# Moving the operands of a split fp32 product to one common place in their 512-byte blocks

## The chip, the cores and the metric

The kernel runs on one core of a Trainium2 chip. The metric is device time in microseconds (us) of one execution. A core has TensorE (PE; its weight loads are listed as PEld), VectorE (DVE), ScalarE (ACT), GpSimd (POOL), and the DMA queues, most of which SyncE (SP) issues to here. SBUF, the on-chip memory, has 128 partitions; a tile takes the same range of bytes in each of them, and "place" here means where in its partition's bytes a tile begins, counted within blocks of 512 bytes.

## The reference, cut to what matters

Two layers work on 256 latent tokens `x` and 256 context tokens `ctx`, with 1024 features. Layer 0 is retention and a dense SwiGLU on all 512 tokens; layer 1 is gated linear attention (GLA) and a mixture of experts on the latent tokens alone, two of eight experts for each token. All is fp32.

```python
h_l = rmsnorm(lat, norm_mix_g[i]) * (1.0 + sc1_l) + sh1_l
...
f = swiglu(h_all, ffn_w_gate[j], ffn_w_up[j], ffn_w_down[j])       # layer 0, width 2816
f = moe_swiglu(h_all, moe_w_router[j], moe_w_gate[j], moe_w_up[j], moe_w_down[j])   # layer 1, 8 x 3584
...
def swiglu(h, w_gate, w_up, w_down):
    return (jax.nn.silu(h @ w_gate) * (h @ w_up)) @ w_down
```

## The kernel before

**A product.** An fp32 product is made of three products of another 4-byte type (fp32r). Each operand is split into a high part and the rest: `whi` and `wlo` of a weight tile, `hh` and `hl` of the normed tokens, `ah` and `al` of the hidden layer, and so on. `mm3` (L87 to L89) issues high x high, high x low and low x high into one PSUM bank. In each, the stationary operand has 128 columns (512 bytes of a partition) and the moving one mostly 512 columns (2048 bytes), sometimes 256.

**A weight tile.** Each 1 MB tile is loaded on SP's queue into a `raw` buffer (`wraw`, L61), cast into `whi` by ScalarE (L79) and subtracted into `wlo` by VectorE (L80), both in `wsplit`. There are four `raw` buffers (in the expert stage three more, tag `more`, and some borrowed places), three `whi` and three `wlo`. The order of the engines' work is the order in which the program issues it; a few lists of pieces (`weave`, `todo`, `ada_beat`) put small work between the products.

**The stages**, by the profiled span: conditioning and retention up to about 412 us, the dense feed-forward up to about 813, GLA up to about 1010, routing, and from about 1047 us the experts (`moe`). An item of the expert loop is one expert and 512 of its 3584 hidden columns: six weight tiles, 72 products, and four transposes (L1417). In the experts' products the weights are the moving operand and the gathered tokens (`hh` or `xb`) or `ah`, `al` the stationary one; in retention and the feed-forward it is mostly the other way round. Tokens of two experts at a time are gathered by products with a one-hot matrix (L1372), and an expert's result goes back by products with `yy` and `GG` (L1460).

**Where tiles lie.** The pools take memory in the order in which their tiles are first asked for; each tile is rounded up to 32 bytes. `cp` and `wp` lie at the bottom, then come the pools of the stage (`rp` retention, `fp` feed-forward, `gp` and `gc` GLA, `mp` and `xp` experts), one after the other over the same bytes. `ap`, with `x0`, `x1`, `hh`, `hl` in that order, stands at the upper end and is pushed down by whatever is added to it. `gap` (L34) asks for a tile that nothing uses. With `reuse_waits="tile"`, the first writer of a tile waits for the last readers of just those tiles whose bytes it takes over.

The sizes of the tiles, added up in this order, give the place of each operand of a split product:

| operand | stage | byte of its block before |
|---|---|---|
| `raw`, `whi`, `wlo` | all | 96 |
| `raw` buffers of tag `more` (no product reads them) | experts | 320 |
| `hh`, `hl`, and over them `xb`, `spare`, GLA's gated outputs | all | 480 |
| `GG`, `yy` (over `x0`, `x1`) | experts | 480 |
| `vh`, `vl`, `pch`, `pcl`, `qh`, `ql`, `kh`, `kl`, `ol` | retention | 96 |
| `plh`, `pll`, `oh` | retention | 224 |
| `ah`, `al` | feed-forward | 480 |
| `ah`, `al` | experts | 480 |
| `th`, `tl` | experts | 224, 352 |
| `wa`, `wuh`, `aT` | GLA | 480 |

Of the kernel before, what the change touches and what calls it, by code (L numbers as in the profile page):

```python
# [8 lines left out]
F32 = mybir.dt.float32  # L9
F32R = mybir.dt.float32r  # L10
# [3 lines left out]
P = 128  # L14
D = 1024
KT = D // P
# [10 lines left out]
def tile_hybrid(ctx: ExitStack, tc: tile.TileContext, a, out):  # L27
# [4 lines left out]
    state = {"pieces": 2}  # L32

    def gap(pool, nbytes):  # L34

        pool.tile([P, nbytes // 4], F32, name=f"gap{state.setdefault('gaps', 0)}")
        state["gaps"] += 1


# [50 lines left out]


    gap(cp, 32)
    tp = ctx.enter_context(tc.tile_pool(name="tp", bufs=3))
    pro = ExitStack()
# [32 lines left out]
    ap = act.enter_context(tc.tile_pool(name="ap", bufs=1, side="right", reuse_waits="tile"))  # L127
    xs = [ap.tile([P, KT, 256], F32, tag=f"x{i}", name=f"x{i}") for i in range(2)]
    hh = ap.tile([P, KT, NTOK], F32R, name="hh")
    hl = ap.tile([P, KT, NTOK], F32R, tag="hl", name="hl")  # L130
    vecT = cp.tile([P, 128], F32, name="vecT")
    wrt = cp.tile([P, KT, 8], F32, name="wrt")
    adabT = cp.tile([P, 96], F32, name="adabT")
# [6 lines left out]

    def gain(layer, which, base_col, A=None, ks=slice(0, KT), streams=2):

        A = A or cp.tile([P, KT, 2], F32, name=f"A{layer}{which}")
        n = ks.stop - ks.start
        g = vecT[:, base_col + ks.start:base_col + ks.stop].unsqueeze(2).to_broadcast([P, n, streams])
        sc = mods[layer][:, which * 24 + 8 + ks.start:which * 24 + 8 + ks.stop, :streams]
        nc.vector.scalar_tensor_tensor(A[:, ks, :streams], sc, 1.0, g, OP.add, OP.mult)
        return A

# [111 lines left out]
    class Norm:  # L261


        def __init__(self, layer, which, A, stream):
            self.layer, self.which, self.A, (self.s, self.sl) = layer, which, A, stream
            self.adder = nc.gpsimd
# [110 lines left out]
    with ExitStack() as ph:  # L377
# [29 lines left out]
        A = cp.tile([P, KT, 2], F32, name="A00")  # L407
# [15 lines left out]
        pro.close()  # L423
        edge = Boundary(0, 1, 32, STREAMS[::-1])
        retention(tc, nc, a, locals(), new_ps, wsplit, wraw, rows, mm3, add_gated)
        edge2 = Boundary(1, 0, 24, STREAMS)
        ffn(tc, nc, a, locals(), new_ps, wsplit, rows, mm3, add_gated)
        tail = gla(tc, nc, a, locals(), new_ps, wsplit, rows, mm3, add_gated)
        moe(tc, nc, a, out, locals(), new_ps, wsplit, rows, mm3)
        act.close()  # L430

# [19 lines left out]
def retention(tc, nc, a, env, new_ps, wsplit, wraw, rows, mm3, add_gated):  # L451
# [3 lines left out]
    with ExitStack() as ph:  # L455
        rp = ph.enter_context(tc.tile_pool(name="rp", bufs=1, reuse_waits="tile"))
# [197 lines left out]
        state = env["state"]  # L654
# [14 lines left out]
        for _ in steps:  # L669
            pass  # L670
        nc.sync.dma_start(rope, a["k_rope"])
        env["gap"](rp, 32)
        lg = rp.tile([P, 2, 4], F32, name="lg")
        nc.scalar.activation(lg, ld, AF.Exp)
        nc.vector.tensor_scalar(lg, lg, -1.0, None, OP.mult)
# [28 lines left out]
def ffn(tc, nc, a, env, new_ps, wsplit, rows, mm3, add_gated):  # L704
    hh, hl, tp = (env[k] for k in ("hh", "hl", "tp"))
    wg, wu, wd = (a["ffn_w_" + n][0] for n in ("gate", "up", "down"))
    with ExitStack() as ph:
        fp = ph.enter_context(tc.tile_pool(name="fp", bufs=2, reuse_waits="tile"))
        nc.sync.dma_start(env["wrt"], a["moe_w_router"][0].rearrange("(k p) e -> p k e", p=P))

        def up(c):
            ws = [wsplit(rows(w, 0, D, c * 256, 256)) for w in (wg, wu)]
            ah = fp.tile([P, 2, NTOK], F32R, tag="ah", name="ah")
            al = fp.tile([P, 2, NTOK], F32R, tag="al", name="al")
            banks = [[new_ps(), new_ps()] for _ in range(2)]
            for part, cols in enumerate([slice(0, 256), slice(256, 512)] if c == 0 else [slice(0, 512)]):
                ts = [tp.tile([P, NTOK], F32, tag="sq", bufs=2, name="t")[:, cols] for _ in range(2)]
                for n, (wh, wl) in enumerate(ws):
                    for m in range(2):
                        ms = slice(m * 128, m * 128 + 128)  # L720
                        ps, t = banks[n][m][:, cols], ts[m]
                        for kt in range(KT):
                            mm3(ps, wh[:, kt, ms], wl[:, kt, ms], hh[:, kt, cols], hl[:, kt, cols],
                                kt == 0, kt == KT - 1)
                        env["ada_beat"](5.12)
                        if c == 0 and part == 0:
                            env["edge"].after(2 * n + m)
                        if n == 0:
                            i = nc.scalar.activation(t, ps, AF.Silu)
                            if c == DFF // 256 - 1 and m == 1:  # L730
                                env["root_table"](i)
                        else:
                            nc.vector.tensor_tensor(t, t, ps, OP.mult)
                            nc.scalar.copy(ah[:, m, cols], t)
                            nc.vector.tensor_sub(al[:, m, cols], t, ah[:, m, cols].bitcast(F32))
            return ah, al

        def down(cs, acts):
            ws = [wsplit(rows(wd, c * 256, 256, 0, D)) for c in cs]
            last = len(cs) > 1  # L740
            for n, part in enumerate([[st] for st in env["edge2"].order] if last else [STREAMS]):
                cols = slice(min(sl.start for _, sl in part), max(sl.stop for _, sl in part))
                for mt in range(KT):
                    ps = new_ps()
                    ms = slice(mt * 128, mt * 128 + 128)
                    k = 2 * len(cs)
                    for ft in range(k):
                        wh, wl = ws[ft // 2]
                        ah, al = acts[ft // 2]
                        mm3(ps[:, cols], wh[:, ft % 2, ms], wl[:, ft % 2, ms], ah[:, ft % 2, cols], al[:, ft % 2, cols],  # L750
                            ft == 0, ft == k - 1)
                    env["ada_beat"](1.28)
                    add_gated(mt, ps, 0, 1, part)
                    if last:
                        env["edge2"].before(n, mt)

        prev = None
        n = DFF // 256
        for c in range(n):
            cur = up(c)  # L760
            if c == 1:
                env["ada_until"](12)
            if prev is not None and c < n - 1:
                down([c - 1], [prev])
            if c == 0:
                env["ada_plan"]([(0, c) for c in range(11, 12)] + [(1, c) for c in range(12)], 3, 2, env["edge"].second.ends[1:])
            if c == n - 1:
                env["ada_until"](0)
                down([c - 1, c], [prev, cur])
            prev = cur  # L770
# [328 lines left out]
def moe(tc, nc, a, out, env, new_ps, wsplit, rows, mm3):  # L1099
    hh, ap, tp, ident, mods = (env[k] for k in ("hh", "ap", "tp", "ident", "mods"))  # L1100
    xT = env["xs"][0]
    wrt = env["wrt"]
    E, FE, FC = 8, 3584, 512
# [7 lines left out]
    with ExitStack() as ph:  # L1111
        mp = ph.enter_context(tc.tile_pool(name="mp", bufs=1, reuse_waits="tile"))
        xp = ph.enter_context(tc.tile_pool(name="xp", bufs=2))
        env["state"]["more"] = mp
        km = mp.tile([P, 320], F32, name="km")
        xl = mp.tile([P, 2, D], F32, name="xl")
        g2b = mp.tile([P, D], F32, name="g2b")
        state = env["state"]
# [5 lines left out]
        nc.gpsimd.tensor_copy(one01, one)  # L1124


        A = env["gain"](1, 1, 40, mp.tile([P, KT, 2], F32, name="A11"), streams=1)

        aw = mp.tile([P, KT * E + 24], F32, name="aw")
        nc.gpsimd.memset(aw, 0.0)  # L1130
        nc.vector.tensor_tensor(aw[:, :KT * E].rearrange("p (k e) -> p k e", e=E), wrt,
                                A[:, :, 0:1].to_broadcast([P, KT, E]), OP.mult)
        w3 = mp.tile([P, 4, 2], F32, name="w3")
        env["gap"](mp, 64)

        def rstd():

# [42 lines left out]
                return k.ins  # L1180
            return pss, add

        th = mp.tile([P, 2, D], F32R, name="th")
        turned = []
        norm = env["Norm"](1, 1, A, STREAMS[0])
        norm.adder = nc.vector
# [62 lines left out]

        state["pieces"] = 1  # L1250
        state["ready"] = ready
        lg = mp.tile([P, 2, E], F32, name="lg")
        for tt in range(2):
            nc.vector.scalar_tensor_tensor(lg[:, tt, :], ps[:, tt * E:tt * E + E], r[:, tt:tt + 1], cb, OP.mult, OP.add)

        env["gap"](mp, 32)
        tl = mp.tile([P, 2, D], F32R, name="tl")

        def normed_high(q):

# [43 lines left out]
                                                OP.mult, OP.add).ins  # L1304
        cmax = mp.tile([1, 1], F32, name="cmax")
        cint = mp.tile([1, 1], mybir.dt.int32, name="cint")
        env["gap"](mp, 32)

        def late():
            with env["held"]([state["split"].ins, state["lost"].ins]):  # L1310
# [18 lines left out]
        env["state"]["pp"] = ph.enter_context(tc.tile_pool(name="pm", bufs=8, space=bass.MemoryType.PSUM, reuse_waits="tile"))  # L1329
        env["state"]["banks"] = 6  # L1330

        env["gap"](mp, 96)
        xs = [hh]
        GG = ap.tile([P, KT, 256], F32R, tag="x0", name="GG")

# [337 lines left out]
```

## Time and profile before

| | |
|---|---|
| median of three runs | 2074.34 us (2073.31 to 2074.95) |
| the profiled execution | 2069.22 us |
| its span, first to last instruction | 2067.5 us |
| instructions in the span | 25718 |
| PE, DVE, ACT busy | 98%, 83%, 56% of the span |
| DMA | 498.22 MB, mean 241 GB/s |

The profiled execution is one more run with the hardware profiler on. "Busy" of PE counts a product from its start to an end that is modelled: products overlap, so that 98% is not a rate. The DMA rate is about 60 to 300 GB/s in the first half of the span and about 350 GB/s in the experts' half.

### The profile page before, as it was taken

Reading aid. Unit: us, or ns where it says so; the run is one execution under the profiler, and the core shown is the slowest. Engines: PE = TensorE matmul, PEld = TensorE weight load, DVE = VectorE, ACT = ScalarE, POOL = GpSimd, SP = SyncE. Lnnn points to the kernel's source line nnn. Section 1 sums busy time; section 2 is a strip of 40 time slices with the busy share of each in tenths; the row PEclk is TensorE's granted clock in tenths of the full one; section 3 lists DMA queues with packets and bytes.
Section 4 is the critical chain, followed back from the end, with each engine's and each line's share of the span. In section 5 each row is a group of like instructions: output and inputs, shape, how many; then the busy total and the mean of one; then the engine's idle time right before and its main releaser. Section 6 shows DMA issues by size and latency. Waiting matters only on the chain.

```text
span 2067.5 us, 25718 instructions
## 1 busy us (share of the span) xinstructions
PE 2018.7 (98%) x9810; PEld 1664.8 (81%) x9810; DVE 1714.8 (83%) x2484; ACT 1162.5 (56%) x1242; POOL 113.8 (6%) x118
## 2 busy tenths in 40 slices
PE   7999999999999999999999999999999999999997
PEld 5788888888888888888878888777887778878775
DVE  5999977659999974687688888888888898888887
ACT  4643434243222223665477777767777677776765
POOL 0201010020000001100110101000000001000000
PEclk9999999999999999999999999999999999999999
DMA  9645343213546662223669899999999999999993
GB/s 286 194 152 186 125 160 102 82 62 123 169 159 222 208 208 68 87 82 104 251 231 358 292 342 356 338 345 360 352 342 345 352 354 351 347 343 358 354 351 139
DMA packets 272498, 498.22 MB, mean 241 GB/s; under 512 B 10357, under 2 KB 112173, under 8 KB 272369
## 3 DMA queue, kind: packets, MB, share of 16 engines
q1 hardware_dynamic: 270976, 495.07, 68.8%
q8 instruction: 79, 1.29, 0.3%
q0 software_dynamic: 512, 0.86, 0.1%
q10 hardware_dynamic: 880, 0.59, 0.1%
q14 instruction: 51, 0.41, 0.1%
HBM read 495.43 MB, written 1.05 MB: 240 GB/s over the span
## 4 chain that ended last, share of the span: by engine, by line
PE 89%; DVE 6%; ACT 2%; issue 1%; DMA 1%; SPq 1%; POOL 0%; ACTq 0%; DVEq 0%; POOLq 0%
PE ps L88 23%; PE ps L87 23%; PE ps L89 23%; PE y L88 5%; PE y L87 5%; PE y L89 5%; DVE wlo L80 3%; PE ps L1417 1%; PE ps L1372 1%; PE ps L975 1%; PE ps L1460 1%; SPq L155 1%; ACT whi L79 0%; PE ps L911 0%; DMA early<-in_ada_w_dram 0%
## 5 line engine op out<-in xcount | busy, mean ns | idle before, releaser
L80 DVE TENSOR_TENSOR wlo<-raw,whi 128x2048 fp32r<-128x2048 f32 (+3 forms) x515 | 933.1, 1832 | 149.1 <-ACT whi L79 145.3
L79 ACT CAST whi<-raw 128x2048 fp32r<-128x2048 f32 (+3 forms) x515 | 784.6, 1541 | 411.4 <-PE ps L88 188.0
L87 PE MATMUL ps<-hh,whi 128*128 128x512 f32 (+1 forms) x864 | 312.0, 363 | 2.1 <-ACT hh L1016 1.0
L89 PE MATMUL ps<-hh,wlo 128*128 128x512 f32 (+1 forms) x864 | 311.0, 361 | 1.7 <-DVE wlo L80 1.7
L88 PE MATMUL ps<-hl,whi 128*128 128x512 f32 (+1 forms) x800 | 292.9, 367 | 2.5 <-DVE hl L322 2.5
L87 PE MATMUL ps<-whi,hh 128*128 128x512 f32 x640 | 256.2, 400 | 1.1 <-ACT hh L321 0.9
L88 PE MATMUL ps<-wlo,hh 128*128 128x512 f32 x640 | 255.1, 399 | 1.6 <-DVE wlo L80 1.6
L214 DVE SCALAR_TENSOR_TENSOR sum<-raw,cT,sum 128x256 f32<-128x256 f32 x448 | 194.2, 484 | 0.4
L89 PEld LDWEIGHTS ps<-hh,wlo 128*128 128x128 f32 x864 | 165.6, 192 | 28.1 <-DVE wlo L80 2.9
L87 PEld LDWEIGHTS ps<-hh,whi 128*128 128x128 f32 x864 | 165.0, 192 | 28.2 <-ACT hh L321 1.5
L88 PE MATMUL ps<-wlo,xb 128*128 128x512 f32 x448 | 180.5, 403 | 3.8 <-DVE wlo L80 3.5
L88 PE MATMUL y<-wlo,ah 128*128 128x512 f32 (+1 forms) x450 | 177.4, 394 | 0.0
L89 PE MATMUL y<-whi,al 128*128 128x512 f32 (+1 forms) x450 | 177.1, 394 | 0.0
L87 PE MATMUL ps<-whi,xb 128*128 128x512 f32 x448 | 177.1, 395 | 0.0
L89 PE MATMUL ps<-whi,hh 128*128 128x512 f32 x448 | 176.7, 394 | 0.0
L89 PE MATMUL ps<-whi,xb 128*128 128x512 f32 x448 | 176.6, 394 | 0.0
L88 PEld LDWEIGHTS ps<-hl,whi 128*128 128x128 f32 x800 | 152.9, 191 | 28.5 <-DVE hl L322 3.4
L87 PE MATMUL y<-whi,ah 128*128 128x512 f32 (+1 forms) x450 | 164.4, 394 | 0.0
L88 PEld LDWEIGHTS ps<-wlo,hh 128*128 128x128 f32 x640 | 121.0, 189 | 30.1 <-DVE wlo L80 4.4
L87 PEld LDWEIGHTS ps<-whi,hh 128*128 128x128 f32 x640 | 120.8, 189 | 29.9 <-ACT hh L321 1.3
L372 DVE SCALAR_TENSOR_TENSOR x<-ps,mod,x 128x256 f32<-128x256 f32 x240 | 105.2, 477 | 37.8 <-PE ps L89 35.8
L88 PEld LDWEIGHTS ps<-wlo,xb 128*128 128x128 f32 x448 | 84.3, 188 | 28.1 <-DVE wlo L80 10.7
(373 smaller groups left out, 2860.0 us busy)
## 6 DMA issues: line engine op xcount, KB each, us to landing
raw<-in_moe_w_gate_dram SPq DMA_DIRECT2D x108, 1024.0 KB, 7.3
raw<-in_moe_w_up_dram SPq DMA_DIRECT2D x108, 1024.0 KB, 7.0
raw<-in_moe_w_down_dram SPq DMA_DIRECT2D x107, 1024.0 KB, 6.9
raw<-in_ada_w_dram SPq DMA_DIRECT2D x44, 1024.0 KB, 5.3
raw<-in_ret_w_in_dram SPq DMA_DIRECT2D x22, 1024.0 KB, 5.3
raw<-in_gla_w_in_dram SPq DMA_DIRECT2D x12, 1024.0 KB, 5.3
raw<-in_ffn_w_gate_dram SPq DMA_DIRECT2D x11, 1024.0 KB, 5.3
raw<-in_ffn_w_up_dram SPq DMA_DIRECT2D x11, 1024.0 KB, 5.4
```

What stands on the lines that cost most here:

```text
L79: state["split"] = nc.scalar.copy(hi[:, ks, ns], raw[:, ks, ns])
L80: state["lost"] = lo_engine.tensor_tensor(lo[:, ks, ns], raw[:, ks, ns], hi[:, ks, ns].bitcast(F32), OP.subtract)
L87: nc.tensor.matmul(ps, lh, rh, start=first, stop=False)
L88: nc.tensor.matmul(ps, lh, rl, start=False, stop=False)
L89: state["mm"] = nc.tensor.matmul(ps, ll, rh, start=False, stop=last).ins
L155: nc.sync.dma_start(t, rows(a["ada_w"][layer], 0, D, c0 + i * n // 2, n // 2))
L214: nc.vector.scalar_tensor_tensor(t, raw[:, k, :], w, t, OP.mult, OP.add)
L372: i = nc.vector.scalar_tensor_tensor(xs[s][:, mt, :], ps[:, sl.start - off:sl.stop - off], g, xs[s][:, mt, :], OP.mult, OP.add)
L975: nc.tensor.matmul(ps[:, h * 256:h * 256 + 256], l, v[:, j, h * 256:h * 256 + 256], start=n == 0, stop=n == 3)
L1372: nc.tensor.matmul(ps, src[:, tt, ks], G[:, tt].rearrange("p e s -> p (e s)"), start=n == 0, stop=n == 3)
L1417: nc.tensor.transpose(ps[:, k * 128:k * 128 + 128], t[:, k * 128:k * 128 + 128], ident)
L1460: nc.tensor.matmul(ps, GT[:, tt, :], ys[i][:, rs, :], start=i == 0, stop=i == 1)
```

## The change

No instruction of the kernel is taken out, added or put elsewhere. The change sets the sizes of the unused `gap` tiles and the order in which `mp`'s tiles are asked for, so that the operands of the split products begin at byte 96 of a block: `hh`, `hl`, `xb`, `GG`, `yy` by the gap behind `hl`; `plh`, `pll`, `oh` by the larger gap in `rp`; the feed-forward's `ah`, `al` by a gap ahead of them; the experts' `th`, `tl` by asking for them right behind two tables of 64 bytes; the experts' `ah`, `al` by the last gap in `mp`. The `raw` buffers of tag `more` come to byte 448; `wa`, `wuh`, `aT` stay at 480. Behind the change the last tile of `xp` ends where `ap` begins.

```diff
     def gap(pool, nbytes):
 
-        pool.tile([P, nbytes // 4], F32, name=f"gap{state.setdefault('gaps', 0)}")
+        pool.tile([P, nbytes // 4], F32, name=f"gap{state.setdefault('gaps', 0)}", bufs=1)
         state["gaps"] += 1
...
     hl = ap.tile([P, KT, NTOK], F32R, tag="hl", name="hl")
+    gap(ap, 384)
...
         nc.sync.dma_start(rope, a["k_rope"])
-        env["gap"](rp, 32)
+        env["gap"](rp, 416)
...
         fp = ph.enter_context(tc.tile_pool(name="fp", bufs=2, reuse_waits="tile"))
+        env["gap"](fp, 128)
...
         env["state"]["more"] = mp
+        A11 = mp.tile([P, KT, 2], F32, name="A11")
+        lg = mp.tile([P, 2, E], F32, name="lg")
+        th, tl = (mp.tile([P, 2, D], F32R, name=n) for n in ("th", "tl"))
         km = mp.tile([P, 320], F32, name="km")
...
-        A = env["gain"](1, 1, 40, mp.tile([P, KT, 2], F32, name="A11"), streams=1)
+        A = env["gain"](1, 1, 40, A11, streams=1)
...
         w3 = mp.tile([P, 4, 2], F32, name="w3")
-        env["gap"](mp, 64)
...
-        th = mp.tile([P, 2, D], F32R, name="th")
         turned = []
...
-        lg = mp.tile([P, 2, E], F32, name="lg")
         for tt in range(2):
             nc.vector.scalar_tensor_tensor(lg[:, tt, :], ps[:, tt * E:tt * E + E], r[:, tt:tt + 1], cb, OP.mult, OP.add)
-
-        env["gap"](mp, 32)
-        tl = mp.tile([P, 2, D], F32R, name="tl")
...
         cint = mp.tile([1, 1], mybir.dt.int32, name="cint")
-        env["gap"](mp, 32)
...
-        env["gap"](mp, 96)
+        env["gap"](mp, 352)
         xs = [hh]
```

## Rows read from the trace of the kernel before

**Rows 1.** Cores: span and mean granted clock.

```profile
core 0: 2067.5 us, clock 0.989
```

**Rows 2.** The chain that ended last, by engine.

```profile
PE 89%; DVE 6%; ACT 2%; issue 1%; DMA 1%; SPq 1%; POOL 0%; ACTq 0%; DVEq 0%; POOLq 0%
```

**Rows 3.** Windows: busy (count) of PE, PEld, DVE, ACT, POOL; clock; DMA; GB/s.

```profile
500.00:600.00 100.00, 100.00 (x435) 81.18 (x435) 96.26 (x213) 24.30 (x30) 0.00 (x0) 1.00 0.49 159
1200.00:1400.00 200.00, 199.26 (x901) 161.31 (x900) 170.43 (x102) 145.55 (x109) 13.35 (x10) 1.00 0.97 347
```

**Rows 4.** Groups by shape: count | busy us, mean ns | idle before.

```profile
L87 PE MATMUL ps<-whi,hh 128*128 128x512 f32 x640 | 256.2, 400 | 1.1 <-ACT hh L321 0.9 <-ACT u L610 0.2
...
L87 PE MATMUL ps<-hh,whi 128*128 128x512 f32 x576 | 227.9, 396 | 0.1
...
L88 PE MATMUL ps<-wlo,xb 128*128 128x512 f32 x448 | 180.5, 403 | 3.8 <-DVE wlo L80 3.5
...
L88 PE MATMUL y<-wlo,ah 128*128 128x512 f32 x446 | 176.3, 395 | 0.0
...
L87 PE MATMUL ps<-hh,whi 128*128 128x256 f32 x288 | 84.0, 296 | 2.0 <-ACT hh L1016 1.0 <-ACT hh L321 1.0
```

**Rows 5.** Timeline of PE, feed-forward, first and last (81 steps): start, duration in us.

```profile
520.73 0.40 PE L87 MATMUL ps<-hh,whi 128*128 128x512 f32 x1
...
539.55 0.39 PE L87 MATMUL ps<-hh,whi 128*128 128x512 f32 x1
```

**Rows 6.** Timeline of PE, experts, first and last (44 steps).

```profile
1399.08 0.39 PE L87 MATMUL ps<-whi,xb 128*128 128x512 f32 x1
...
1409.30 0.40 PE L89 MATMUL ps<-whi,xb 128*128 128x512 f32 x1
```

**Rows 7.** Timeline of PE, retention, after 0, 6 and 17 steps.

```profile
109.03 0.39 PE L87 MATMUL ps<-vh,pch 128*128 128x512 f32 x1
...
110.42 0.39 PE L87 MATMUL ps<-vh,pch 128*128 128x512 f32 x1
...
112.91 0.40 PE L89 MATMUL ps<-vh,pcl 128*128 128x512 f32 x1
```

**Rows 8.** Timeline of PE, retention's scores, first and last (6 steps).

```profile
267.74 0.39 PE L87 MATMUL ps<-qh,kh 128*128 128x512 f32 x1
...
269.10 0.28 PE L87 MATMUL ps<-qh,kh 128*128 128x256 f32 x1
```

**Rows 9.** Timeline of PE, retention's output products, first and last (27 steps).

```profile
169.26 0.39 PE L87 MATMUL ps<-oh,whi 128*128 128x512 f32 x1
...
175.44 0.39 PE L87 MATMUL ps<-oh,whi 128*128 128x512 f32 x1
```

**Rows 10.** Timeline of PE, GLA, 256 columns, first and last (33 steps).

```profile
929.87 0.28 PE L87 MATMUL ps<-hh,whi 128*128 128x256 f32 x1
...
933.79 0.28 PE L87 MATMUL ps<-hh,whi 128*128 128x256 f32 x1
```

**Rows 11.** Timeline of PE, retention, 256 columns, first and last (5 steps).

```profile
165.42 0.28 PE L88 MATMUL ps<-ql,kh 128*128 128x256 f32 x1
...
166.02 0.40 PE L87 MATMUL ps<-qh,kh 128*128 128x512 f32 x1
```

**Rows 12.** Waits, 1047 to 2050 us: total us, times, longest.

```profile
ACT whi L79 <- PE ps L89: 92.6, 134, 1.8
...
PEld ps L88 <- DVE wlo L80: 14.9, 22, 0.9
...
PE ps L88 <- DVE wlo L80: 5.1, 20, 0.5
```

**Rows 13.** Groups by shape, 1047 to 2050 us, the two halves of a split.

```profile
L80 DVE TENSOR_TENSOR wlo<-raw,whi 128x2048 fp32r<-128x2048 f32 x303 | 687.4, 2288 | 96.7 <-ACT whi L79 96.2
L79 ACT CAST whi<-raw 128x2048 fp32r<-128x2048 f32 x303 | 577.1, 1909 | 138.2 <-PE ps L89 83.5 <-PE y L89 52.9 <-DVE t L1411 1.8
```

**Rows 14.** Waits of the whole span.

```profile
POOL km L1119 <- PE ps L1009: 171.1, 1, 171.1
```

## The prediction

> **What bounds the kernel now.** I read the chain that ended last first. TensorE holds 89% of it, VectorE 6%, DMA 1% [rows 2]. The windows by stage say the same: in the dense feed-forward stage TensorE is busy 100.00 us of 100, in the expert stage 199.26 of 200 [rows 3]. In the second window the DMA share is 0.97 at 347 GB/s, so transfers are the one resource that looks as full. The waits of that stage answer this: ScalarE's casts wait for TensorE to give a weight buffer back (92.6 us in 134 waits on one group alone), TensorE waits for the subtraction `wlo` in 22 places (its weight loads 14.9 us, the products right behind them 5.1 us more), and no row of that list names a DMA [rows 12]. The weights lie landed in `raw` until TensorE frees a `whi`; the DMA queue is paced by TensorE. So a change of TensorE's rate is a change of the time.
>
> How fast TensorE is can't be read from the mean durations: the 512-column products show 395 to 403 ns each [rows 4], but these ends are modelled and overlap. The starts are what counts. Between two starts of the same line far apart, divided by the count, lies the true step. Feed-forward stage: 18.82 us for 81 steps, 232.3 ns [rows 5]. Expert stage, where the weights are the streamed operand: 10.22 us for 44 steps, 232.3 ns [rows 6]. In both, one operand starts at byte 96 and the other at byte 480 of its block (`whi`, `wlo` against `hh`, `hl`, `xb`, `ah`, `al`).
>
> The kernel already has products whose two operands start at the same byte, 96: retention's `vh`, `vl` against `pch`, `pcl`. They begin at 232 ns a step (109.03 to 110.42 us, six steps) and then settle: 110.42 to 112.91 us is 2.49 us for 11 steps, 226.4 ns [rows 7]. The scores (`qh`, `kh`, all at 96) run 1.36 us for 6 steps, 226.7 ns, from the first on [rows 8]. A third distance, `oh` at 224 beside `ol` and the weights at 96, gives 6.18 us for 27 steps, 228.9 ns [rows 9]. The clock doesn't make the difference: it is 1.00 in the windows of the two slow stretches [rows 3] and 0.989 over the whole span [rows 1]. The shape is the same too. What differs among the three is where the operands start. I take 226.6 ns as the settled step of equal places.
>
> **The change part by part.** No instruction is added, removed or reordered. Tiles move.
>
> 1. `gap(ap, 384)`: the pool `ap` stands at the upper end of the memory, so 384 bytes behind `hl` push `x0`, `x1`, `hh`, `hl` down from byte 480 to byte 96. With them go `xb`, `GG`, `yy` and GLA's gated outputs, which reuse these places. `gap(fp, 128)` does it for the feed-forward's `ah`, `al`, the 352 in `mp` for the experts' `ah`, `al`. Products that change from 480/96 to 96/96, by the groups of the page's longer list: 2 of 640, 3 of 576, 4 of 448, 3 of 446 (one of each in [rows 4]), and 192 + 3 x 144 smaller ones of the same kind: 1280 + 1728 + 1792 + 1338 + 192 + 432 = 6762. At 232.3 - 226.6 = 5.7 ns each: **-38.5 us**.
>
> 2. `gap(rp, 416)`: `plh`, `pll`, `oh` from 224 to 96. The output products are 288 at 512 columns: 288 x (228.9 - 226.6) = **-0.7 us** [rows 9].
>
> 3. Restarts. A stretch does not settle at once: the one above spent six steps at 231.7, 5.1 ns too much each, 31 ns [rows 7]; the scores spent nothing [rows 8]. I take 30 ns, bounds 0 and 60. Every item of the expert loop is broken once by its transposes (56), 22 waits break it again [rows 12], some 32 scatters and gathers lie between, and I estimate 50 breaks ahead of the expert stage: 160 x 30 ns = **+4.8 us** (0 to 9.6).
>
> 4. The 256-column products. With places 480/96 they step at 3.92 us / 33 = 118.8 ns [rows 10], with equal places at 0.60 us / 5 = 120 ns [rows 11]. Here the change costs. About 1376 of them: 288 + 288 + 224 + 64 of `hh`, `hl` (the first in [rows 4]), six groups of 64 of `oh`, `ol`, `ah`, `al`, and 128 of the gather: x 1.2 ns = **+1.7 us**; the five steps are few and rounded to 10 ns, so 0 to 3.
>
> 5. Waits in the expert stage. TensorE gives a buffer back, ScalarE casts (1.91 us), VectorE subtracts (2.29 us) [rows 13], and TensorE needs the result some 4.2 us later, 18 of its own steps. Where TensorE already waits, those 18 steps get shorter by 18 x 5.7 = 0.10 us and the wait longer by the same: 22 x 0.10 = **+2.3 us**. Lower bound 0; upper bound 9, four times that, if places that now just escape a wait get one too and if VectorE has a scatter's addition queued ahead of the subtraction, which makes the chain longer. In the feed-forward stage VectorE is busy 96.26 of 100 us [rows 3], and TensorE's 100 would become 97.6: still the longer one, so I cost it at nothing. If that cover goes, VectorE's 96.3 is the floor.
>
> 6. The order of tables in `mp`: `A11`, `lg`, `th`, `tl` go ahead of `km`, `xl`, `g2b`, so each lies over other tiles of GLA than before and waits for other last readers. `th`, `tl` come to lie over `q`, `kl`, which the transposes at L1009 read last; the load of `km` waited for these (171.1 us on GpSimd, in which it had nothing else to do [rows 14]) and now lies over `L`, whose readers end sooner. `th` is first written in the router's part, behind the output products that follow that line. I cost it at nothing; GpSimd's queue behind `km` holds the copies for `up01`, `one01` and the memset of `aw`, and if they came later the router's products would. The spare `raw` buffers go from 320 to 448; no product reads them, and the casts and subtractions take what they take from any place.
>
> Sum: -38.5 - 0.7 + 4.8 + 1.7 + 2.3 = **-30.4 us**. The profiled execution took 2069.2 us around its span of 2067.5 us [rows 1]; it becomes 2069.2 - 30.4 = 2038.8 us. The median of the runs lies 5.1 us above the profiled one, which the profile doesn't explain and I carry over: 2074.3 - 30.4 = 2043.9, so **2044 us**.
>
> A page speaks against this sum. The Trainium skill, "TensorE: Matmul & The Clock Gate", gives the start-to-start step of a warm product as N/2.4 + 2.5 ns, 215.7 ns at 512 columns ("Wait — 56ns, not 53.3ns?"), and lets the next weights load through a read port of their own, without taking bandwidth from the running product ("Step-by-step: what each phase is for"). By that rule the place of an operand is no term and the sum is 0. The trace differs twice: the step is 232.3 ns in both long stretches [rows 5, 6], and 226.4 where the places are equal [rows 7].
>
> **The rivals.**
> - *It never settles in long stretches.* The stretch of equal place is followed over 17 steps only; restart included, it is 3.88 us / 17 = 228.2 ns [rows 7]. If the restart comes back all the time, the gain is 6762 x 4.1 = 27.7 us, less 1.7 and 2.3: 23.7 us, **2051 us**. For it: the 22 waits and the transposes. Against it: they leave stretches of some 30 to 70 products. 15%.
> - *The chain through ScalarE and VectorE takes over in the expert stage.* That stage holds 4 x 448 + 448 + 448 + 3 x 446, 4026 of the 6762 products (the two single 448s are its share of the 640s); the others are 2736 x 5.7 = 15.6 and the 0.7, less 3 for restarts and 256-column products: 13 us, **2061 us**. The same figure stands if DMA at 0.97 can't go faster. For it: the 22 waits, VectorE 170 of 200 us [rows 3]. Against it: 15% of VectorE is still idle there, and most waits are ScalarE's for TensorE. 8%.
> - *Nothing happens* because 226.6 belongs to the retention stage (its short operands, its calm engines) and not to the place: **2074 us**. Against it: `oh` and `ol` sit in that same stage at 228.9, the weights among them. 6%. The skill's two independent read ports would have it so.
> - *Slower: equal places make the two reads meet.* The 256-column products are 1% slower at equal places [rows 10, 11], and the six restart steps are at 231.7. If long stretches at 512 columns got the 1%, they would step at 234.6: 6762 x 2.3 = 15.6 + 1.7, **2091 us**. It decides from a mean step above 232.3 ns on. Against it: eleven steps in a row at 226.4. 5%.
>
> **How the numbers follow.** The forecast has 66%, on its own 2037 (no loss but the 256-column products) to 2056 (restarts, waits and 256-column products at their upper bounds). With the first rival it is 81%. The upper end reaches 2062 to take in the second (89%), since the tails of all three fall outside the ends. Faster by over 0.2% (4.1 us, about what a measurement of this kernel can tell): 66 + 15 + 8 = 89%; within 0.2%: 6%; slower: 5%.
>
> **What would show it.** Right: starts in the feed-forward and the expert stage at 226 or 227 ns in long rows; the first five or so after each transpose at up to 236; 256-column steps near 120; TensorE's waits for `wlo` a few us longer; DMA share in the expert stage up and GB/s near 355. Wrong: a step of 228 or more that repeats inside a stretch (rival one), waits for `wlo` over 30 us (two), 232 as before (three), over 232.3 (four). Wrong also if VectorE holds up the feed-forward stage or the expert stage starts later, by a wait for the moved tables.

## The result

The changed kernel takes **2041.61 us** (median of 4 runs, 2040.36 to 2042.96) against 2074.4 us for the kernel before in the same comparison (2073.31 to 2074.95). The ratio is 0.9843, with a 95% interval of 0.9826 to 0.986: 32.8 us faster, where 2044 us, or 30 us faster, were forecast. Measured again beside later versions the ratio was 0.9862 (0.9844 to 0.9879), 28.3 us; the two intervals overlap. The profiled execution took 2042.05 us around a span of 2040.3 us, 27.2 us less than that of before.

First the cores, the chain that ended last by engine, and the windows of the same two stretches as in [rows 3] (busy time and count of PE, PEld, DVE, ACT, POOL; granted clock; DMA share; GB/s), all of the kernel after:

```profile
core 0: 2040.3 us, clock 0.988
```

```profile
PE 88%; DVE 7%; ACT 2%; issue 2%; DMA 1%; SPq 1%; POOL 0%; ACTq 0%; DVEq 0%; POOLq 0%
```

```profile
500.00:600.00 100.00, 100.00 (x445) 82.80 (x445) 98.10 (x219) 24.97 (x31) 0.00 (x0) 1.00 0.55 177
1200.00:1400.00 200.00, 198.91 (x916) 163.91 (x915) 173.12 (x103) 147.60 (x111) 13.73 (x10) 1.00 0.98 355
```

TensorE still sets the end, and as nearly alone as before [rows 2]. The clock is the same as before to 0.001 [rows 1]. In the same 100 us of the feed-forward stage TensorE works off 445 products in place of 435, in the same 200 us of the expert stage 916 in place of 901, and the DMA queue follows: 355 GB/s at a share of 0.98, where 347 and 0.97 stood [rows 3]. So the transfers did go faster when TensorE asked for them sooner. VectorE is now busy 98.10 us of the 100 in the feed-forward stage (96.26 before), so little is left there before it would set the pace.

The groups by shape (count, busy time, mean duration) show once more that the mean duration of a product is not its step. They lie within 3 ns of [rows 4]:

```profile
L87 PE MATMUL ps<-whi,hh 128*128 128x512 f32 x640 | 254.3, 397 | 0.3 <-ACT u L611 0.3
...
L88 PE MATMUL ps<-wlo,xb 128*128 128x512 f32 x448 | 179.0, 400 | 4.6 <-DVE wlo L80 4.5
...
L87 PE MATMUL ps<-hh,whi 128*128 128x256 f32 x288 | 84.1, 296 | 2.0 <-ACT hh L1018 1.0 <-ACT hh L322 0.9
```

The timeline of PE does show it (start, duration in us). In the feed-forward stage a stretch begins behind two small products at 505.05 us:

```profile
505.05 0.30 PE L185 MATMUL psada<-rows,base 128*128 128x32 f32 x2
...
505.50 0.39 PE L88 MATMUL ps<-al,whi 128*128 128x512 f32 x1
...
507.58 0.39 PE L88 MATMUL ps<-al,whi 128*128 128x512 f32 x1
...
531.83 0.39 PE L87 MATMUL ps<-hh,whi 128*128 128x512 f32 x1
```

From 505.50 to 507.58 us there are 9 steps in 2.08 us, 231 ns; from there to 531.83 us 107 steps in 24.25 us, **226.6 ns**, without one of them over 227. [Rows 5] had 232.3 over 81 steps. In the expert stage the first pair of rows spans 59 steps in 13.37 us, again 226.6 ns where [rows 6] had 232.3; then come the four transposes (the row of `base,t`), and the stretch begins anew:

```profile
1385.01 0.39 PE L88 MATMUL ps<-wlo,xb 128*128 128x512 f32 x1
...
1398.38 0.40 PE L87 MATMUL ps<-whi,xb 128*128 128x512 f32 x1
1398.62 0.60 PE L1415 MATMUL ps<-base,t 128*128 128x128 f32 x4
...
1399.28 0.39 PE L89 MATMUL ps<-whi,xb 128*128 128x512 f32 x1
...
1400.66 0.39 PE L89 MATMUL ps<-whi,xb 128*128 128x512 f32 x1
```

1399.28 to 1400.66 us is 6 steps at 230 ns, then 226 and 227 again. The output products of retention settle as well, with `oh` now at byte 96: the rows below span 27 steps in 6.12 us, 226.7 ns, for the 228.9 of [rows 9]. The 256-column products of GLA span 26 steps in 3.12 us, 120.0 ns, for the 118.8 of [rows 10]:

```profile
171.13 0.39 PE L88 MATMUL ps<-ol,whi 128*128 128x512 f32 x1
...
177.25 0.39 PE L88 MATMUL ps<-ol,whi 128*128 128x512 f32 x1
```

```profile
920.07 0.28 PE L87 MATMUL ps<-hh,whi 128*128 128x256 f32 x1
...
923.18 0.28 PE L89 MATMUL ps<-hh,wlo 128*128 128x256 f32 x1
```

Last the waits of the expert stage (in total, times, longest) and the two halves of a split, for [rows 12, 13], and GpSimd's wait ahead of the load of `km`, for [rows 14]:

```profile
ACT whi L79 <- PE ps L89: 83.4, 114, 2.1
...
PEld ps L88 <- DVE wlo L80: 15.7, 22, 0.9
...
PE ps L88 <- DVE wlo L80: 6.3, 21, 0.5
```

```profile
L80 DVE TENSOR_TENSOR wlo<-raw,whi 128x2048 fp32r<-128x2048 f32 x303 | 686.4, 2288 | 85.2 <-ACT whi L79 84.8
L79 ACT CAST whi<-raw 128x2048 fp32r<-128x2048 f32 x303 | 577.6, 1911 | 127.8 <-PE ps L89 74.7 <-PE y L89 49.6 <-DVE t L1409 0.8
```

```profile
POOL km L1124 <- PE ps L1011: 148.9, 1, 148.9
```

ScalarE waits 9 us less for TensorE, TensorE waits 2.0 us more for `wlo` (22.0 for 20.0 us). The cast and the subtraction take the same time to 2 ns. Of their operands the change moves only the `raw` buffers of tag `more`; with the weights' tiles at byte 480, in the second experiment below, they take 1911 and 2288 ns too. So only TensorE's products were seen to depend on the place. `km` came loose earlier in its wait (148.9 for 171.1 us), and nothing followed from it.

Since both kernels run the same 9810 products in the same order, the time can be followed product by product. I added the start-to-start steps of all split products (a step of more than 245 ns at 512 columns, or 135 at 256, is a break, and what it has above that limit goes to the breaks):

| us | before | after | difference |
|---|---|---|---|
| 7298 products of 512 columns | 1697.5 | 1663.6 | -33.9 |
| 1484 products of 256 columns | 178.1 | 179.5 | +1.4 |
| breaks in these | 47.2 | 50.9 | +3.7 |
| everything else | 128.0 | 129.7 | +1.7 |
| from the first product to the last | 2050.9 | 2023.6 | -27.2 |

### The profile page after: what moved, and what is told of

The parts are those of the page before. It is cut to its first block, busy times and chain, and to the rows that moved or that the text cites. A ratio compares the mean times of both kernels' runs of the same rounds, so it can differ in the third digit from the quotient of the medians.

```text
span 2040.3 us, 25721 instructions
## 1 busy us (share of the span) xinstructions
PE 1987.9 (97%) x9810; PEld 1665.2 (82%) x9810; DVE 1711.3 (84%) x2484; ACT 1163.1 (57%) x1242; POOL 116.7 (6%) x118
## 4 chain that ended last, share of the span: by engine, by line
PE 88%; DVE 7%; ACT 2%; issue 2%; DMA 1%; SPq 1%; POOL 0%; ACTq 0%; DVEq 0%; POOLq 0%
PE ps L88 23%; PE ps L87 22%; PE ps L89 22%; PE y L88 5%; PE y L89 5%; PE y L87 5%; DVE wlo L80 3%; PE ps L1415 1%; PE ps L1370 1%; PE ps L977 1%; SPq L156 0%; PE ps L1458 0%; ACT whi L79 0%; PE ps L913 0%; DMA early<-in_ada_w_dram 0%
```

## The experiments

**Bare products at pairs of places.** A kernel that does none of the reference's work: stretches of 42 fp32r products, nothing else beside them, the moving operand at one place and the stationary one at another, 512 columns and then 256. It was executed once, at a granted clock of 0.999.

```python
for cols in (512, 256):
    for m, s in PLACES:          # (96, 96 + d) for d in 0, 32 .. 480, and four more
        for i in range(42):
            k, j = i % 7, i % 6
            nc.tensor.matmul(ps[:, 0:cols], still[:, s + j * 128:s + j * 128 + 128],
                             moving[:, m + k * 512:m + k * 512 + cols], ...)
```

> This kernel does none of the reference's work. It streams stretches of 42 products each, one after the other, with a moving and a stationary operand at 21 pairs of places, first with 512 columns and then with 256. Theory (the distance between the two places sets the step): 226 to 227 ns at every equal pair (96/96, 0/0, 480/480, 224/224), 232 ns where the two lie 384 bytes apart, other steps at other distances; at 256 columns 120 ns at equal places, 119 ns at 384 apart. Rival (each operand's own crossing of a block's border sets it): 0/0 is the fastest, below 226 ns, 480/480 and 96/96 differ from it. Rival (the place is no term and the feed-forward's 232 ns came from the engines working beside it): all 42 stretches at one step for each width.

The name of a stretch gives the columns, the byte of the moving operand and that of the stationary one. The timeline of PE groups neighbours of one kind: start of the first, time to the end of the last, count. Here are the ends of seven stretches:

```profile
203.05 6.97 PE L37 MATMUL psw512m0s0x<-moving,still 128*128 128x512 f32 x30
...
56.78 7.16 PE L37 MATMUL psw512m96s160x<-moving,still 128*128 128x512 f32 x30
...
95.93 7.03 PE L37 MATMUL psw512m96s288x<-moving,still 128*128 128x512 f32 x30
...
249.69 3.68 PE L37 MATMUL psw256m96s160x<-moving,still 128*128 128x256 f32 x31
...
324.23 3.88 PE L37 MATMUL psw256m0s0x<-moving,still 128*128 128x256 f32 x31
...
259.43 3.84 PE L37 MATMUL psw256m96s224x<-moving,still 128*128 128x256 f32 x31
...
319.08 3.88 PE L37 MATMUL psw256m480s96x<-moving,still 128*128 128x256 f32 x31
```

Thirty products of 512 columns take 6.97 us at equal places, 7.16 with the weights 64 bytes above and 7.03 at 192; 31 of 256 columns take 3.68 us at 64 and 3.88 at equal places. The last one's modelled end is in each of these. The mean steps of the last 28 of the stretches with the moving operand at 96, from the starts:

| stationary minus moving, mod 256 | 0 | 32 | 64 | 96 | 128 | 160 | 192 | 224 |
|---|---|---|---|---|---|---|---|---|
| 512 columns, ns | 226.7 | 233.3 | 233.3 | 234.3 | 232.4 | 233.3 | 228.9 | 233.4 |
| 256 columns, ns | 120.0 | 118.3 | 113.3 | 120.0 | 118.8 | 120.0 | 117.7 | 117.7 |

Both operands at 0, at 224 or at 480 give 226.6 to 226.7 as well, so at 512 columns what counts is the distance and neither the place itself nor the border of a block that an operand crosses. The steps of the kernel before stand in this table: 480 against 96 is 128 mod 256, 232.4 and 118.8 ns [rows 5, 6, 10]. One bare stretch does not fit: at 256 columns the moving operand at 480 and the weights at 96, the very places of [rows 10], took 120.0 ns (the last line above), where 96 and 224, also 128 apart, took 118.8. So at 256 columns neither the distance nor the two places fix the step closer than some 1 ns. The output products, whose 228.9 I took for a distance of their own, mixed 128 (`oh`) and 0 (`ol`) [rows 9]; two of three at 232.4 and one at 226.7 would make 230.5, so a mixed stretch is not the mean of its parts either. Two things no theory had: the pattern repeats after 256 bytes, not after 512, and at 256 columns the best distance is 64, while equal places are among the slowest.

**All operands at another common byte**, 480, by a gap of 416 bytes ahead of the weights and none behind the tokens:

```diff
-    gap(cp, 32)
+    gap(cp, 416)
...
-    gap(ap, 384)
```

> The changed kernel with all operands of its split products at byte 480 in place of 96 (a larger gap ahead of the weight buffers, none behind the tokens). Theory (equal places): as the changed kernel, 2041 us within 4, steps of 226 to 227 ns in the expert and the feed-forward stage. Rival (byte 96 itself, or where an operand crosses a block's border): not the same, most of the 33 us lost, 2065 to 2075 us.

2041.86 us (2039.83 to 2044.4), ratio 0.9861 (0.9846 to 0.9876): the changed kernel's time. Stage by stage its trace agrees with the changed kernel's within some 2 us.

**Only the tokens' tiles**, the kernel before with the one gap behind `hl`:

```diff
     hl = ap.tile([P, KT, NTOK], F32R, tag="hl", name="hl")
+    gap(ap, 384)
```

> The kernel before with the one gap behind the tokens' low half, so that only the tokens' tiles and what reuses their places come to byte 96; both stages' hidden operands stay at 480, three of retention's at 224. Theory (the gain is a sum over products): 4992 of the 6762 products change, 4992 x 5.7 = 28.5 us, less 3.5 for restarts, 1.7 for 256 columns and 2 for waits: 21 us, 2053 us. Rival (the gain needs all streams at one place, since each switch between unequal places starts the settling again): the expert items alternate between both kinds every 48 and 24 products, and the gain falls below 15 us, 2060 us or more.

2050.68 us (2048.7 to 2051.69) against 2071.7 us for the kernel before on that chip, ratio 0.9896 (0.9881 to 0.9911): 21.0 us, as worked out. One place of its expert stage has both kinds side by side, the `up` products with equal places and the `down` products, whose `ah` and `al` were left at 480. Timeline of PE:

```profile
1388.38 0.39 PE L87 MATMUL ps<-whi,xb 128*128 128x512 f32 x1
...
1396.54 0.39 PE L87 MATMUL ps<-whi,xb 128*128 128x512 f32 x1
...
1397.70 0.39 PE L88 MATMUL y<-wlo,ah 128*128 128x512 f32 x1
...
1401.64 0.39 PE L88 MATMUL y<-wlo,ah 128*128 128x512 f32 x1
```

36 steps in 8.16 us, 226.7 ns; then 17 in 3.94 us, 231.8 ns. The rate changes from one product to the next with the operand.

**Only the order of the tables**, all other places as before (`th` and `tl` come to byte 96; the three small gaps among these tables go, and the last gap in `mp` keeps `ah`, `al` at 480):

```diff
+        A11 = mp.tile([P, KT, 2], F32, name="A11")
+        lg = mp.tile([P, 2, E], F32, name="lg")
+        th, tl = (mp.tile([P, 2, D], F32R, name=n) for n in ("th", "tl"))
         km = mp.tile([P, 320], F32, name="km")
...
-        env["gap"](mp, 96)
+        env["gap"](mp, 224)
```

> The kernel before with the new order of the experts' tables alone; every operand of a split product but the gather's two moving tables stays at its old place. Theory (the order costs nothing): within 2 us of the kernel before, 2074 us, and the wait ahead of the router's first product with the chosen experts is as before, 1.7 us from start to start. Rival (the tables wait for other readers of the bytes that they take over): this wait is 2.3 us as in the changed kernel, and the routing is some 1 us later.

2070.78 us (2067.78 to 2073.11, 11 runs) against 2071.7, ratio 0.9997 (0.9988 to 1.0006). The order costs and brings nothing that can be measured. In its trace the first product with `selm` waits 1.5 us for VectorE, in the profile of before 1.3, in that of after 2.0, so the longer wait there is not the order's. The second profile of the changed kernel has 1.2, so it is not the change's either.

**The tokens 256 bytes away from the rest**:

```diff
-    gap(ap, 384)
+    gap(ap, 128)
```

> The changed kernel with the distance behind the tokens' tiles 128 bytes in place of 384: these tiles then begin 256 bytes from the weights and the other operands (places 352 against 96 of a 512-byte block). If equal places in a 256-byte block are what counts, as the stretch of bare products showed (226.7 ns at a distance of 256), the time is that of the changed kernel, about 2041 us, and the steps of feed-forward and experts settle at 226.7 again. If the 512-byte block is what counts, the 4992 products of 512 columns that have one operand from these tiles take about 232 ns, +26 us, about 2068.

2040.53 us (2039.04 to 2042.14), ratio 0.9855 (0.9839 to 0.9872), with the changed kernel at 2041.4 beside it (its own expectation stands below, with the faster version). In its trace 1617 of the 1728 feed-forward products with moving `hh` or `hl` step at 226 or 227 ns. Operands at 352 and 96 of a 512-byte block are as good as equal ones: the 256-byte period holds in the kernel.

**The tokens 64 bytes away**:

```diff
-    gap(ap, 384)
+    gap(ap, 320)
```

> The changed kernel with the distance behind the tokens' tiles 320 bytes in place of 384: these tiles then begin 64 bytes above the weights. By the stretch of bare products the sign counts: where the tokens are stationary (3264 products of 512 columns: values of retention and of GLA, gate and up of the experts) the step is 233.3 in place of 226.64, +21.7 us; where they move (1728 products of 512 columns) 228.9, +3.9 us; some 1000 products of 256 columns with moving tokens take 117.75 for 120, -2.2 us; together about +23 us, 2064 us. If only the size of the distance counted, at 228.9 for all, it is about +9 us, 2050; at 233.3 for all +31 us, 2072.

2056.87 us (2056.72 to 2058.09), ratio 0.9934 (0.9918 to 0.995): 15.5 us more than the changed kernel, between the 9 of "size alone" and the 23 of "sign counts". The timeline of PE decides. The first pair of rows lies in the feed-forward stage, where the tokens move; the second in the expert stage, where they are stationary:

```profile
520.54 0.39 PE L87 MATMUL ps<-hh,whi 128*128 128x512 f32 x1
...
527.40 0.39 PE L87 MATMUL ps<-hh,whi 128*128 128x512 f32 x1
```

```profile
1392.36 0.40 PE L89 MATMUL ps<-whi,xb 128*128 128x512 f32 x1
...
1395.86 0.39 PE L89 MATMUL ps<-whi,xb 128*128 128x512 f32 x1
```

30 steps in 6.87 us, 228.9 ns; 15 in 3.50 us, 233.4 ns. Both are the values of the table, so the sign counts. The sum was too large in part because I counted from 226.64, the settled step, while the changed kernel's products of the expert stage with stationary tokens average 228.2 with their restarts, and at the distance of 64 there is nothing left to lose in a restart: 2688 of them went from 228.2 to 233.2, 13.4 us, not 17.9. That is 4.5 of the 7.5 us by which it missed; another 2 lie between the medians and the profiled executions, which are 17.5 us apart, and the rest was not traced.

**A faster version: GLA at its own distance.** The table says that GLA's 256-column products should have the weights 64 bytes above the tokens. GLA alone gets a view of the tokens' tiles 64 bytes lower, mod 256; all else stays equal mod 256.

```diff
-    hh = ap.tile([P, KT, NTOK], F32R, name="hh")
-    hl = ap.tile([P, KT, NTOK], F32R, tag="hl", name="hl")
-    gap(ap, 384)
+    hhs = ap.tile([P, KT * NTOK + 48], F32R, name="hh")
+    hls = ap.tile([P, KT * NTOK + 16], F32R, tag="hl", name="hl")
+    hh, hl, hh1, hl1 = at(hhs, 0), at(hls, 16), at(hhs, 48), at(hls, 0)
+    gap(ap, 128)
...
+            hi, lo = (hh1, hl1) if self.layer else (hh, hl)
```

> The changed kernel, but in the GLA stage both copies of the tokens lie 64 bytes lower, so that the stationary weights begin 64 bytes above the moving tokens; everywhere else the places are equal as in the changed kernel (the tile of the tokens is 64 or 192 bytes larger, and the distance behind it is smaller). In the measurement of the pairs of places, 256 columns took 113.3 ns at this distance and 120.0 at equal places, and 512 columns took 228.9 ns at the opposite one (64 bytes below) against 226.64. Theory (the distance modulo 256 bytes alone sets the step): 672 products of 256 columns with weights of 96 at 113.3 for 120.0 is -4.5 us, 192 products of the values at 228.9 for 226.64 is +0.4 us, so about -4.1 us against the changed kernel in the same call, some 2037.5 us, and the step of the GLA rows is 113 ns. First rival (113.3 ns belongs to the bare stretch of products and does not come in a kernel whose other engines read and write): no gain, +0.4 us. Second rival (in the GLA stage the score levels on VectorE set the end): the steps fall to 113 ns but the stage keeps its time, waits growing by what the products save, within 1 us of the changed kernel.

> The changed kernel as it is, in the same call as the versions made from it, so that they are compared on one chip. Every theory expects the ratio of its first comparison again, about 0.984, and some 2041 us.

2036.12 us (2033.62 to 2037.99) against 2041.4 (2039.8 to 2043.6) for the changed kernel on the same chip; against the kernel before 0.9833 (0.9818 to 0.9848). All its runs lie below all of the changed kernel's: 5.3 us. Timeline of PE in GLA:

```profile
914.47 0.28 PE L89 MATMUL ps<-hh,wlo 128*128 128x256 f32 x1
...
918.77 0.28 PE L88 MATMUL ps<-hl,whi 128*128 128x256 f32 x1
```

38 steps in 4.31 us, 113.3 ns. The mean over GLA's products of this kind is 114.4 ns (119.8 in the changed kernel), and adding all steps, GLA and the router's stage got 3.2 us shorter by them. The other 2 us lie in breaks of the feed-forward stage, which differ by as much between two executions of equal places (that stage took 373.9 us here and at the common byte 480, 375.0 and 376.2 in the two profiles of the changed kernel), so I don't put them down to the edit.

**Which two operands?** Again bare products, executed once, at a granted clock of 1.00. The moving operand's place goes round three values, and the stationary one's follows at once, one product later or two.

```python
m, s = places[i % 3], places[(i - shift) % 3]   # shift 0 "own", 1 "next", 2 "second"
```

> Stretches of 42 bare fp32r products again, none of the reference's work. First, which two operands' places count: the places go round three values (96, 128, 160 in the near stretches, 96, 160, 224 in the far ones), and the stationary operand's place follows the moving one's at once (own), one product later (next: the weights of the product after begin where the present moving operand begins), or two products later (second). If what counts is a product's own two operands, the own stretches settle at 226.6 ns for 512 columns (120 for 256) and the two others at the mean of unequal distances, near 231 to 233 for 512. If it is the moving operand against the weights that are loaded beside it for the product after, the stretches called next settle at 226.6 and the own ones near 231 to 233; if two products ahead, those called second. Then 384 and 128 columns at distances of 0 to 224 bytes: if the best distance is always zero, 384 columns are fastest at 0; if it goes with the number of columns, as 0 for 512 and 64 for 256 suggest, it lies elsewhere. The period of 256 bytes gives no forecast of the size, some 3 per cent of a step by the nearest stretches.

No theory held. At 512 columns the near stretches took 231.2 (own), 233.3 (next) and 231.2 ns (second), the far ones 230.0, 233.3 and 232.6; none came to 226.6. At 256 columns they took 117.6, 117.7 and 120.2, the far ones 120.2, 117.7 and 117.7. Timeline of PE, the last 30 products of the near stretches at 512 columns (own, next, second), to be read against the 6.97 us above:

```profile
37.55 7.10 PE L38 MATMUL psownnear512x<-moving,still 128*128 128x512 f32 x30
...
47.28 7.16 PE L38 MATMUL psnextnear512x<-moving,still 128*128 128x512 f32 x30
...
57.06 7.10 PE L38 MATMUL pssecondnear512x<-moving,still 128*128 128x512 f32 x30
```

It is not enough that a product's own operands agree, or those of a product and its neighbour: of the stretches tried, only those whose place stayed the same came to 226.6. Which accesses meet stays open: the runs show that the distance sets the step, not why. With fixed places, 384 columns took 173.3 to 173.4 ns at distances 0, 32, 96 and 192, 174.6 at 64, 175.8 at 128 and 176.6 at 160 and 224; 128 columns took 111.6 to 111.8 at every distance.

## Why the prediction was right

It forecast faster by the first mechanism, 2044 us, and the kernel came 2.4 us below that. That this is so close is partly luck. The forecast is 2038.8 us for the profiled execution and 5.1 us on top, by which the median of before lay above its profiled execution. The profiled execution came to 2042.05, 3.2 us more, as the span fell by 27.2 us and not by 30.4; and the median lies 0.4 us below it, not 5.1 above. The 5.1 was scatter and nothing to carry over: executions of the kernel before spread from 2068.29 to 2075.67 us in the later comparisons. The two misses have opposite signs. By medians the gain was 32.8 and 28.3 us in two comparisons, with 30.4 between them. By its own steps:

- *What bounds the kernel.* Right. Of what the 512-column products saved, most reached the end: 17.3 of 18.5 us in the expert stage, 6.7 of 7.3 in the feed-forward (5.5 in a second profile of the same kernel). DMA and the split followed.
- *Steps 1 to 3, the 512-column products.* -38.5 - 0.7 + 4.8 = -34.4 us were forecast, -33.9 measured. The parts hold too: 7298 x 226.67 is 1654.2 us, so restarts and other short disturbances cost 9.4 us in the kernel after. Restarts run longer than the six steps of [rows 7]: nine in the feed-forward rows above. Before, the same sum by the settled steps (6762 at 232.3, 288 at 228.9, 248 at 226.6) is 1692.9, so 4.6 us of such losses were there already. The difference, 4.8 us, is the term. That it agrees to the tenth is chance, since 0.1 ns more in the settled step of before is 0.7 us.
- *Step 4, the 256-column products.* +1.7 forecast, +1.4 measured, at 120.0 ns as taken from five steps.
- *Step 5, waits.* +2.3 forecast. TensorE's waits for `wlo` grew by 2.0 us by the list of waits; by the steps, the breaks of the expert stage by 1.2.
- *Step 6, the order of tables.* Nothing forecast; the experiment that did it alone measured 0.9997.
- *What wasn't in the sum.* Some 4 us of the profiled execution: breaks and other work outside the expert stage. Between 25 and 60 us the granted clock was 0.88 (0.96 before), and over the whole trace 18 products of 512 columns stepped at 422 to 429 ns, 11 before. The second profile has 0.95 in that window and 9 such products, and from the first split product to the end of retention it is 2.1 us shorter (0.8 us from the first product of all), so this part is scatter between executions. At the router the change looks to blame at first: TensorE's wait for `selm` grew from 1.3 to 2.0 us, and behind it 22 of the gather's 256-column products stepped at 213 to 214 ns where 10 did before (nearly all the rest are at 112 to 125), at a granted clock of 0.50, that is its lower level of 1.2 GHz: 12 x 0.094 = 1.1 us. But the second profile has 1.2 us and 20 products, and the one at the common byte 480 has 1.4 us and 9. So these differences too come and go between executions with equal places, and none is shown to be the change's.
- *The rivals.* "It never settles" fell with 107 steps in a row at 226 or 227; what is right in it is that restarts recur; they are within the 9.4 us. "The chain through ScalarE and VectorE takes over" fell: the expert stage became 17.3 us shorter (981.6 to 964.3, from the first product into `y` to the last). "Nothing happens" and "slower" fell; the mean step went down, not up, though at 256 columns equal places are indeed among the worst distances.

The rule of the Trainium skill, "TensorE: Matmul & The Clock Gate", section "Wait — 56ns, not 53.3ns?", would give 215.7 ns a product. No run here shows it for fp32r at 512 columns: the best was 226.6, in bare stretches too, and the place of the operands moved it up to 234.3. Nor does the table of distances agree with the two independent read ports of the same page of the Trainium skill ("Step-by-step: what each phase is for"): the step moves with the distance between the two operands.

## What to carry to other kernels

Where TensorE is the bound and a profile shows steps that differ between stretches of the same shape, list the start bytes of both operands and of the stretch's other products before anything else; a gap of a few hundred bytes moved 1.6% here. The best distance depends on the number of columns (0 at 512, 64 at 256, none at 128, mod 256 bytes), and bare stretches lost it when the place moved from product to product, so choose one place by stage. Count the gain from starts, not durations, and subtract a restart of some six to nine steps for every break.

## What was not expected of the hardware

- At 512 columns the pattern of distances repeats after 256 bytes, in bare stretches (226.7 ns at 0 and at 256 apart) and in the kernel (2040.53 us at 256 apart, 2041.4 at 0).
- At 256 columns the weights 64 bytes above the moving operand give 113.3 ns a product, 5.6% less than equal places; 128 columns at 111.6 ns are hardly faster than that, so at this distance the step hardly falls any more from 256 to 128 columns.
- Equal places within each product are not enough if the place moves from one product to the next: 230.0 to 231.2 ns at 512 columns in place of 226.6.
